# One transformer layer on one core: halves of the array, six warm products, a new order

## The chip, the cores and the metric

The kernel runs on one core of a Trainium2 chip. A core has five engines with a queue each: TensorE (PE, matrix products; its weight loads are shown as PEld), VectorE (DVE), ScalarE (ACT), GpSimd (POOL) and SyncE (SP), whose queue issues most DMAs here. Products write to PSUM, which has eight banks of 128 partitions by 2 KB; everything else lives in SBUF, 128 partitions too. The metric is the time of one execution in microseconds (us) on the device, the median of several runs; lower is better.

## What is computed

One decoder layer in float32, 512 tokens of width 1024, with 256 memory tokens:

```python
h = swiglu(rms_norm(x, ffn1_pre_norm[l]), ffn1_w_gate[l], ffn1_w_up[l], ffn1_w_down[l])
x = x + 0.5 * rms_norm(h, ffn1_post_norm[l])
u = rms_norm(x, mix_pre_norm[l])
...
k_cmp = compress_blocks(kv[:, :, 0], cmp_pos_k[l], cmp_k_w1[l], cmp_k_w2[l])
v_cmp = compress_blocks(kv[:, :, 1], cmp_pos_v[l], cmp_v_w1[l], cmp_v_w2[l])
...
merged = (gates[:, :, 0] * (o_nsa @ w_branch_nsa[l])
          + gates[:, :, 1] * (o_dn @ w_branch_dn[l])
          + gates[:, :, 2] * (o_mem @ w_branch_mem[l]))
x = x + rms_norm(merged @ w_out[l], mix_post_norm[l])
h = swiglu(rms_norm(x, ffn2_pre_norm[l]), ffn2_w_gate[l], ffn2_w_up[l], ffn2_w_down[l])
x = x + 0.5 * rms_norm(h, ffn2_post_norm[l])
```

Three mixers run on the same normed input `u`: an attention in two groups of four heads of 64 (`o_nsa`: over compressed keys, over all causal keys as selected blocks, and over a window; with 512 tokens all eight blocks of 64 are selected and the window reaches all of them), a gated delta rule with four heads of 128 (`o_dn`), and a cross-attention into the memory (`o_mem`). `compress_blocks` is a small network over blocks of 32 tokens: silu of a product with 2048 x 256 weights, once for keys and once for values, then a second product.

## The kernel before

The layer is written out without loops on the device. Most large products are split in two parts of reduced precision, so that one product is three instructions (L117 to L119, helper `mm3`): high by high, low by high, high by low. Each weight tile of 128 x 512 is loaded (L105), cast to its high part on ACT (L106), and its low part is made on DVE or POOL (L109). Small products stay in fp32, and each shows as two instructions in the trace.

The order of work is given by lists of tasks in the dictionary `PRM`: `order_s` for the start of the first FFN, `order0` for its end, `order` for the delta rule and the projections, `order2` for the attention, the memory attention and the merging of the branches, `order3` for the output product and the passage into the second FFN. `tasks` (L1118) walks such a list; a letter names the task and the digits are its arguments. A planner then places each instruction in its engine's queue: among those whose inputs are ready by its own model of time it takes the one that stands earliest in the program. `off` moves a task's instructions ahead by so many places. `order(later, earlier)` tells the planner that one instruction may be placed only after another; it adds no wait on the chip by itself. `pool` says which share of a task's low parts go to POOL. On the chip each engine's queue then runs in the planned order.

These pieces matter here:

- Start: `__init__` fills a tile `wm` with zeros and multiplies it eight times (L61) while the first loads run; the results are not used. `transp` (L190) transposes the first 256 tokens, two feature blocks of 128 at a time (tasks `t00` to `t03`); the tokens come in two halves of 512 features, the second loaded by task `y`.
- Compressed keys: `cmp_in` (tasks `x`), then `cmp_hid` (L927, tasks `p0` to `p7`). Each `p` task loads two weight tiles of 256 KB (L935), one for keys, one for values, from the ring of buffers of the other weights, and makes four products (L940): for two k steps, keys into PSUM partitions 0 to 63 and values into 64 to 127.
- Attention: tasks `S` (`nsa_soft`, L1031) make scores, softmax and the scaling of the probabilities (L217, four per task); tasks `P` (`nsa_pt`, L1054) transpose the probabilities on PE (L1062) and copy them back (L1065); tasks `V` (`nsa_pv`, L1068) multiply them with the values (L1074). A `V` task takes two `P` results, one per group; for each of four key blocks group 0 writes PSUM partitions 0 to 63 and group 1 writes 64 to 127. There are 16 `S`, 16 `P` and 8 `V` tasks. `W` tasks close a pair of heads, `M` tasks merge a branch into the output (`merge_tile`, 36 instructions on PE each).

Of the kernel before, what the change touches and what calls it, by code (L numbers as in the profile page):

```python
# [36 lines left out]
PRM = {'order': ['i', 'a', 'w', 'c01', 'h01', 'r0', 'c00', 'c10', 'c02', 'l0', 'h00', 'h02', 'c12', 'k0', 'h10', 'c22', 'c11', 'h12', 'h11', 'h22', 'r1', 'k1', 'l1', 'b0', 'c21', 'z', 'h21', 'e0', 'c20', 'r2', 'h20', 'c32', 'l2', 'c31', 'd00', 'h31', 'k2', 'r3', 'd01', 'l3', 'b1', 'd02', 'x0', 's00', 'e1', 'd10', 'c30', 'h32', 'x1', 'd11', 'h30', 's01', 's02', 's03', 'q0', 'q3', 'p0', 'o0', 'p1', 'p2', 'p3', 'k3', 'd12', 's10', 'p4', 'q1', 'p5', 's11', 'p6', 'p7', 's12', 's13', 'o1', 'q2', 'f'], 'dma': {'l': 'sync', 'b': 'sync', 'd': 'scalar', 'c': 'sync', 'r': 'sync'}, 'off': {'b0': 300, 'h31': 400, 'r1': 50, 'h32': 50, 'h11': 200, 'h12': 200, 'd10': 100, 'A01': 100, 'A10': 100, 'A11': 100, 'A20': 400, 'A31': 100, 'A21': 20, 'x0': 20, 'x1': 20, 'L': 200, 'S310': 400, 'S001': 20, 'S311': 400, 'A30': 100, 'r0': 400, 'd02': 20, 's11': 100, 'V20': 400, 'l3': 100, 'q1': 20, 'f': 400, 'l1': 20, 'h20': 100, 'h22': 100, 'r3': 50, 'P010': 50, 'y': 100, 'h02': 50, 'S101': 20, 'A00': 100, 'Q0': 50, 'Q1': 200, 'Q2': 50, 'Q3': 50, 'P110': 400, 'V31': 50, 'd01': 200, 'o0': 400, 'p0': 50, 'p1': 50, 'p2': 50, 'p4': 50, 'p5': 20, 'p6': 50, 'p7': 50, 'b1': 200, 'h01': 100, 'M15': 20, 'P201': 400, 'e0': 100, 'e1': 100, 'o1': 20, 'q0': 50, 'q2': 20, 'h21': 20, 'd11': 50, 'p3': 50, 'U0': 100, 's13': 50, 'c11': 20, 's00': 200, 'P011': 400, 'M14': 200, 'c20': 50, 'k2': 20, 'M03': 20}, 'ph': 'e', 'po': 'ss', 'xpd': (0, 1, 2), 'order2': ['K1', 'K0', 'B', 'M10', 'Q0', 'C0', 'Q1', 'S000', 'C3', 'S001', 'P001', 'P000', 'C1', 'S010', 'C2', 'S011', 'V00', 'P010', 'Q2', 'S101', 'S100', 'P011', 'S110', 'V01', 'P100', 'W0', 'P101', 'S111', 'Q3', 'V10', 'P110', 'M12', 'S200', 'P111', 'V11', 'P200', 'S210', 'M14', 'S201', 'M15', 'P201', 'S211', 'W1', 'V20', 'P211', 'P210', 'V21', 'S301', 'S300', 'W2', 'P301', 'S311', 'M11', 'P300', 'L', 'M13', 'S310', 'G0', 'V30', 'P310', 'M16', 'G2', 'P311', 'M17', 'V31', 'W3', 'A00', 'M00', 'A01', 'G1', 'U0', 'M05', 'A10', 'A11', 'G3', 'A30', 'U1', 'A31', 'U3', 'M03', 'M06', 'A20', 'A21', 'U2', 'M07', 'M22', 'M20', 'M02', 'M24', 'M27', 'M21', 'M23', 'M01', 'M04', 'M26', 'M25'], 'order0': ['d0', 'p0', 'n0', 't0', 'd1', 'k2', 'k0', 'p2', 'p3', 'v', 'k3', 'n1', 'k1', 't1'], 'order3': ['s3', 's7', 's2', 's6', 's1', 's5', 's0', 's4', 'd00', 'd01', 'd11', 'g', 'p0', 'n0', 't0', 'd10', 'p1', 'n1'], 't3': (('mm', 'r'), ('e', 's')), 'pool': {'W2': 2, 's13': 3, 'k0': 0, 'k1': 0, 'k2': 0, 'k3': 2, 'p3': 1, 'C0': 1, 'C1': 0, 'C2': 0, 'C3': 2, 'S310': 0, 'L': 3, 'd11': 3, 'p0': 1, 'p1': 1, 'p2': 1, 'p4': 2, 'p5': 1, 'p6': 1, 'p7': 1, 'S311': 0, 'h01': 0, 'h00': 2, 'h02': 0, 'h10': 0, 'h11': 0, 'h12': 0, 'h22': 0, 'h21': 0, 'h20': 0, 'h31': 0, 'h30': 3, 'h32': 0, 'i': 2, 'P011': 2, 'c21': 0, 'd01': 2, 'S000': 0, 'S001': 0, 'S010': 0, 'S011': 0, 'S100': 0, 'S101': 0, 'S110': 0, 'S111': 0, 'S200': 0, 'S201': 0, 'S210': 0, 'S211': 0, 'S300': 0, 'S301': 0, 'M24': 2, 'G2': 2, 'A01': 0, 'M10': 1, 'M15': 2, 'M12': 2, 'M14': 2, 'M13': 2, 'M17': 2, 'M11': 2, 'M16': 2, 'M23': 0, 'M27': 3, 'M01': 2, 'M00': 2, 'M03': 0, 'M07': 2, 'M06': 1, 'M22': 2, 'M04': 2, 'M20': 2, 'M26': 3, 'M02': 0, 'M21': 2, 'M25': 2, 'M05': 2, 'c11': 1, 'o1': 3, 'P000': 2, 'P001': 1, 'P010': 2, 'P100': 2, 'P101': 2, 'P110': 2, 'P111': 2, 'P200': 2, 'P201': 2, 'P210': 2, 'P211': 2, 'P301': 0, 'P300': 2, 'P310': 2, 'P311': 2, 'c12': 0, 'b1': 1, 'x0': 0, 'x1': 0, 'V21': 0, 'c30': 0, 'c01': 0, 'c02': 0, 'c00': 0, 'c10': 0, 'c22': 0, 'c20': 0, 'c31': 0, 'c32': 0, 's01': 3, 'A31': 0, 'd12': 0, 'y': 2, 'G0': 2, 'G1': 2, 'G3': 0, 'U3': 0, 'W3': 2, 'r1': 2, 's12': 3, 'U2': 0, 'Q0': 2, 'Q1': 2, 'Q2': 2, 'Q3': 1, 's00': 3, 's02': 2, 's03': 3, 's10': 2, 's11': 3, 'e1': 2, 'd00': 1, 'U0': 0, 'U1': 0, 'l2': 0, 'd02': 2, 'K1': 3, 'V11': 0, 'V00': 2}, 'pool3': {'d00': 3, 'd01': 3, 'd10': 3, 'd11': 0, 'p1': 2, 't1': 3, 't0': 3, 's5': 2, 's7': 2, 's1': 2, 's0': 2, 's3': 2, 's6': 2, 's2': 2, 's4': 2, 'q0': 1}, 'pool0': {}, 'off0': {'p3': 20, 'n1': 50, 'd0': 200, 'k2': 400, 'k1': 400}, 'off3': {'s1': 20, 's5': 200, 'g': 200, 't0': 400, 'd10': 200, 'p0': 200}, 'tt': ('e', 's'), 'order_s': ['t00', 'w10', 'w00', 'y', 't01', 't02', 'w01', 't03', 'w11', 'R0', 'F000', 'x', 'F101', 'n', 'F200', 't10', 't11', 't12', 't13', 'c', 'F110', 'B', 'F211', 'F011'], 't0': ('e', 's'), 'rs': ((0, 0), (0, 0)), 'ra': (1, 1), 'warm': 8, 'pools': {'F000': 0, 'F101': 0, 'F200': 0, 'F011': 0, 'F110': 0, 'F211': 0, 'w10': 0, 'w11': 0, 't00': 0, 't01': 0, 't02': 0, 't03': 0, 't13': 0, 't10': 0, 't11': 0, 't12': 0, 'w00': 0, 'w01': 0}, 'ptc': 'vvs', 'cva': 'v', 'offs': {'t13': 100, 'R1': 400, 't03': 20, 'w10': 200}, 'vnc': 's', 'sp3': 0, 'hsc': 'vv', 'sf2': 2, 'psc': 'vvvv', 'sp1': 0, 'vbs': 'v', 't1c': 'vs', 'sgv': 256}  # L37


class Body:  # L40
    def __init__(self, ctx, tc, a, out, tap):
# [12 lines left out]
        wm = self.tp.tile([P, 512], BF16, tag="tmpb", bufs=2, name="wm")  # L54
# [4 lines left out]
        pw = self.bank("o", "warm")  # L59
        for _ in range(PRM.get("warm", 10)):  # L60
            nc.tensor.matmul(pw, wm[:, :P], wm, start=True, stop=True)  # L61
# [10 lines left out]


# [139 lines left out]
    def scale(self, eng, out, src, r):  # L213
        if eng == "s":
            self.nc.scalar.activation(out, src, AF.Copy, scale=r)
        else:
            (self.nc.gpsimd if eng == "g" else self.nc.vector).tensor_scalar(out, src, r, None, op0=OP.mult)  # L217
# [709 lines left out]
    def cmp_hid(self, c, Xs, d):  # L927

        nc = self.nc
        if c == 0:  # L930
            d["ph"] = self.bank(PRM.get("ph", "e"), "phid")[:, :256]
        w1 = []
        for which in range(2):
            w = self.wp.tile([P, 2, 256], F32, tag="wraw", name="w1", bufs=self.WB[0])
            nc.sync.dma_start(w, self.a["cmp_w1"][which, c])  # L935
            w1.append(w)
        for k in range(2):
            m = 2 * c + k
            for which in range(2):
                nc.tensor.matmul(d["ph"][64 * which : 64 * which + 64], Xs[which][:, m].rearrange("p g c -> p (g c)"),  # L940
                                 w1[which][:, k], start=m == 0, stop=m == 15)
# [89 lines left out]
    def nsa_soft(self, i, g, br, A, K, tb, sg, ap_):  # L1031
# [20 lines left out]
        return Pm

    def nsa_pt(self, Pm, ap_):  # L1054
        nc, v, te = self.nc, self.nc.vector, self.nc.tensor
        PT = ap_.tile([P, 1280], F32, tag="PT", name="PT", bufs=2)
        for bank, kbs in enumerate(((0,), (1, 3), (2,))):
            pt = self.bank("s", "ppt")
            o = 0
# [8 lines left out]
    def nsa_pv(self, i, br, po, pts, vt):  # L1068
        te = self.nc.tensor
        col = (0, 512, 1024, 896)  # L1070
        for kb in range(TB):
            n = SEQ - kb * P
            for g in range(2):
                te.matmul(po[64 * g : 64 * g + 64, kb * P :], vt[:, kb, br * P + 64 * g : br * P + 64 * g + 64],  # L1074
                          pts[g][:, col[kb] : col[kb] + n], start=br == 0 and kb == 0, stop=False, skip_group_check=True)
# [51 lines left out]
    def run(self):  # L1127
# [3 lines left out]
        with tc.tile_pool(name="f1", bufs=1) as fp, contextlib.ExitStack() as x1:  # L1131
# [13 lines left out]
            def consts():  # L1145
# [76 lines left out]
        with tc.tile_pool(name="mx", bufs=1) as mp:  # L1222
# [293 lines left out]
```

## Time and profile before

| | before |
|---|---|
| median of 3 runs | 1361.38 us |
| lowest and highest | 1360.89, 1362.07 us |
| profiled execution, its own time | 1360.6 us |
| its span, first to last instruction | 1358.8 us |
| PE, DVE, ACT, POOL busy | 98%, 66%, 53%, 10% of the span |
| HBM traffic | 130 GB/s over the span |

The span is what the trace covers; the rest of the execution's time lies around it. A busy PE is not PE at its peak: matrix products are pipelined, so an instruction's time overlaps the next one's, and the step from start to start says what one costs.

### The profile page before, as it was taken

The numbers are of one execution on the slowest core, as the hardware profiler recorded it, in microseconds if no ns is written. First come the engines' busy times: TensorE is split into PE (matmuls) and PEld (weight loads), VectorE is DVE, ScalarE is ACT, GpSimd is POOL, SyncE is SP. The second block draws the span as 40 slices with busy tenths as digits, with TensorE's granted clock in tenths as the row PEclk, the third lists the DMA queues.
The fourth block names the chain that finished last, engine by engine and source line by source line (L and its number), as shares of the span: only waits on it lengthen the run. The fifth ranks groups of instructions, "written<-read, shape, count | busy, mean of one in ns | idle before, by whom it ended". The sixth has DMA issues, their size and how long they took to land.

```text
span 1358.8 us, 21802 instructions
## 1 busy us (share of the span) xinstructions
PE 1330.2 (98%) x7839; PEld 1128.1 (83%) x7839; DVE 899.9 (66%) x1802; ACT 717.7 (53%) x1538; POOL 142.3 (10%) x129
## 2 busy tenths in 40 slices
PE   8999999999999989999999999999999999999997
PEld 7889999788797778787767777788878899998886
DVE  6897876765768775745887323322688778766775
ACT  6566664765655543316655234333576566646652
POOL 0020000000011322003111112323200000000000
PEclk8999999999999999999999999999999999999999
DMA  7543331586664341423111222533744433317773
GB/s 246 194 149 118 100 119 32 178 255 184 210 187 131 83 124 41 126 95 120 52 47 48 78 62 68 189 95 92 257 139 140 135 122 98 121 33 255 199 223 106
DMA packets 107453, 178.32 MB, mean 131 GB/s; under 512 B 18908, under 2 KB 28496, under 8 KB 107344
## 3 DMA queue, kind: packets, MB, share of 16 engines
q1 hardware_dynamic: 107056, 176.67, 41.9%
q8 instruction: 61, 1.00, 0.3%
q14 instruction: 48, 0.39, 0.1%
q10 hardware_dynamic: 288, 0.26, 0.1%
HBM read 166.84 MB, written 10.01 MB: 130 GB/s over the span
## 4 chain that ended last, share of the span: by engine, by line
PE 88%; DVE 5%; ACT 2%; DMA 2%; issue 1%; POOL 0%; SPq 0%; ACTq 0%; DVEq 0%; POOLq 0%
PE smm L429 10%; PE pfm L117 7%; PE pfm L118 7%; PE pfm L119 7%; PE se L429 7%; PE ss L429 3%; PE po L1074 2%; PE ps L1042 2%; PE acc_e L118 2%; PE acc_e L119 2%; PE acc_e L117 2%; PE sr L429 2%; PE acc_s L119 1%; PE acc_s L117 1%; PE acc_s L118 1%; PE so L429 1%
## 5 line engine op out<-in xcount | busy, mean ns | idle before, releaser
L106 ACT CAST whi<-wraw 128x512 fp32r<-128x512 f32 (+1 forms) x314 | 189.8, 614 | 181.4 <-PE pfm L119 65.1
L109 DVE TENSOR_TENSOR wlo<-wraw,whi 128x512 fp32r<-128x512 f32 (+1 forms) x268 | 183.9, 694 | 125.3 <-ACT whi L106 118.2
L117 PE MATMUL pfm<-xth,whi 128*128 128x512 f32 x384 | 154.5, 405 | 3.0 <-DVE cacc L635 3.0
L118 PE MATMUL pfm<-xth,wlo 128*128 128x512 f32 x384 | 154.2, 405 | 1.0 <-POOL wlo L109 1.0
L119 PE MATMUL pfm<-xtl,whi 128*128 128x512 f32 x384 | 154.5, 405 | 0.0
L117 PEld LDWEIGHTS pfm<-xth,whi 128*128 128x128 f32 x384 | 72.4, 189 | 21.0 <-issue 5.2
L119 PEld LDWEIGHTS pfm<-xtl,whi 128*128 128x128 f32 x384 | 72.4, 188 | 16.3 <-issue 2.0
L118 PEld LDWEIGHTS pfm<-xth,wlo 128*128 128x128 f32 x384 | 72.5, 189 | 16.1 <-POOL wlo L109 1.3
L109 POOL TENSOR_TENSOR wlo<-wraw,whi 128x512 fp32r<-128x512 f32 (+1 forms) x43 | 53.6, 1248 | 221.4 <-ACT whi L106 195.2
L106 ACT CAST ringh<-ringr 128x512 fp32r<-128x512 f32 x82 | 50.1, 620 | 42.8 <-PE acc_e L118 8.4
L429 PE MATMUL smm<-thi,fset 128*128 128x256 f32 x384 | 69.4, 279 | 0.0
L109 DVE TENSOR_TENSOR wlo<-ringr,ringh 128x512 fp32r<-128x512 f32 x75 | 51.3, 689 | 21.2 <-PE acc_e L119 6.8
L429 PEld LDWEIGHTS smm<-thi,fset 128*128 128x128 f32 x384 | 58.5, 188 | 0.2
L445 DVE TENSOR_TENSOR up<-smm,s 128x256 f32<-128x256 f32 x32 | 13.6, 424 | 66.5 <-ACT se L442 66.5
L429 PE MATMUL smm<-thi,fxtl 128*128 128x256 f32 x192 | 53.5, 279 | 0.6 <-DVE fxtl L411 0.6
L429 PE MATMUL smm<-thi,fxth 128*128 128x256 f32 x192 | 53.3, 277 | 0.0
L429 PE MATMUL se<-thi,fset 128*128 128x256 f32 x256 | 46.7, 280 | 0.0
L1045 ACT ACTIVATE Pm<-Pm,nm 128x128 f32<-128x128 f32 (+1 forms) x64 | 35.7, 559 | 15.5 <-DVE nm L1044 14.6
L402 DVE TENSOR_TENSOR fs<-fq 128x1024 f32<-128x1024 f32 x32 | 39.0, 1217 | 0.3 <-DMA fq<-in_ffn_u_dram 0.3
L429 PEld LDWEIGHTS se<-thi,fset 128*128 128x128 f32 x256 | 39.1, 187 | 0.0
L123 DVE TENSOR_TENSOR Hl<-H,Hh 128x256 fp32r<-128x256 f32 x88 | 34.9, 420 | 5.6 <-ACT Hh L122 3.7
L1044 DVE CUSTOM_DVE_ANT_0 Pm<-ps,tbl 128x128 f32<-128x128 f32 (+1 forms) x64 | 29.7, 484 | 10.9 <-PE ps L1042 10.3
(565 smaller groups left out, 3946.5 us busy)
## 6 DMA issues: line engine op xcount, KB each, us to landing
wraw<-in_ffn_d_dram SPq DMA_DIRECT2D x94, 256.0 KB, 2.8
ringr<-in_ffn_d_dram SPq DMA_DIRECT2D x82, 256.0 KB, 3.0
fq<-in_ffn_g_dram SPq DMA_DIRECT2D x64, 256.0 KB, 2.8
fq<-in_ffn_u_dram SPq DMA_DIRECT2D x64, 256.0 KB, 2.6
wraw<-in_w_gate_dram SPq DMA_DIRECT2D x48, 256.0 KB, 2.7
wraw<-in_ffn_u_dram SPq DMA_DIRECT2D x34, 256.0 KB, 3.2
wraw<-in_ffn_g_dram SPq DMA_DIRECT2D x34, 256.0 KB, 2.9
woraw<-in_w_out_dram SPq DMA_DIRECT2D x32, 256.0 KB, 3.0
```

What stands on the lines that cost most here:

```text
L106: nc.scalar.copy(hi, raw)
L109: eng.tensor_tensor(lo, raw, hi.bitcast(F32), op=OP.subtract)
L117: t.matmul(out, lh, rh, start=first, stop=False)
L118: t.matmul(out, ll, rh, start=False, stop=False)
L119: t.matmul(out, lh, rl, start=False, stop=last)
L123: return self.nc.vector.tensor_tensor(lo, src, hi.bitcast(F32), op=OP.subtract)
L402: add = lambda *x: v.tensor_tensor(*x, op=OP.add)
L429: m = lambda x, y, **kw: te.matmul(out, x, y, skip_group_check=True, **kw)
L1042: te.matmul(s[:, : max(n, 256)], A[:, qb * P : qb * P + P], K[j][:, : max(n, 256)], start=j == 0, stop=j == 1)
L1044: v.tensor_tensor_reduce(pm, s[:, :n], tb[:, SEQ - n :], -1.0, 3e38, op0=OP.add, op1=OP.min, accum_out=nm[:, qb : qb + 1])
L1045: nc.scalar.activation(pm, pm, AF.Exp, bias=nm[:, qb : qb + 1], scale=-1.0, accum_out=sm[:, qb : qb + 1])
L1074: te.matmul(po[64 * g : 64 * g + 64, kb * P :], vt[:, kb, br * P + 64 * g : br * P + 64 * g + 64], pts[g][:, col[kb] : col[kb] + n], start ...
```

## The change

Four things are edited.

1. `warm` becomes a method, and the zero tile `wm` gets a place of its own. The new task `H6` in `order_s`, between `t01` and `t02`, makes six more of the unused products.
2. In `cmp_hid` the two weight tiles of a chunk come in one load of 512 KB into a tile of their own with two buffers; the host lays the weights out for it.
3. `scale` returns its instruction. `nsa_pt` orders its first transpose after the last scaling of its probabilities, and `nsa_pv` its first product after the last copies of both `P` results.
4. The task lists `order`, `order2` and `order3`, and several offsets and shares for POOL, are set anew.

```diff
-        pw = self.bank("o", "warm")
-        for _ in range(PRM.get("warm", 10)):
-            nc.tensor.matmul(pw, wm[:, :P], wm, start=True, stop=True)
+        self.warm(PRM.get("warm", 10))
...
+    def warm(self, n):
+        p = self.bank("o", "warm")
+        for _ in range(n):
+            self.nc.tensor.matmul(p, self.wm[:, :P], self.wm, start=True, stop=True)
...
-        w1 = []
-        for which in range(2):
-            w = self.wp.tile([P, 2, 256], F32, tag="wraw", name="w1", bufs=self.WB[0])
-            nc.sync.dma_start(w, self.a["cmp_w1"][which, c])
-            w1.append(w)
+        w1 = d["cm"].tile([P, 2, 2, 256], F32, tag="w1", name="w1", bufs=2)
+        nc.sync.dma_start(w1, self.a["cmp_w1"][c])
...
-        return Pm
+            q = self.scale(PRM.get("psc", "vvvv")[qb], pm, pm, sm[:, qb : qb + 1])
+        return Pm, q
...
+                    if not bank and not o and PRM.get("gp", 1):
+                        self.order(q, after)
...
+                if not kb and not g and PRM.get("gv", 1):
+                    for p in pts:
+                        self.order(q, p[1])
...
+                "H": self.warm,
```

In `PRM` the lists change in these places (offsets: what was, what is; none means zero):

```
order    c11 c22 ahead of h12 (was c22 c11); c21 h21 b0 e0 z (was b0 c21 z h21 e0);
         k2 ahead of l2 (was behind h31); s01 ahead of h30; q3 p0 d12 o0 p1 q0 p2
         (was q0 q3 p0 o0 p1 p2 .. d12 behind k3)
order_s  H6 between t01 and t02
order2   P000 ahead of C3, P010 ahead of C2, M12 ahead of P100, S200 S210 ahead of V10,
         W2 ahead of S300, P301 behind P300, P310 behind M17, A31 U3 ahead of U1, M25 ahead of M04
order3   s2 and s5 earlier, d10 ahead of n0
off      V00 V01 V10 V11 V21 V30: none to 400; V31: 50 to 400
         p1 p2 p3 p4 p6 p7: 50 to 400; p5: 20 to 400
         h00 none to 400; l2, P101 none to 200; i none to 100; h11 200 to 100; l1 20 to 50;
         G0, S210, G2 none to 20
off0     d0 200 to none; k1 400 to 20; p0 none to 400; p2 none to 100
off3     t0 400 to 200; n0 none to 200
```

More of the change, by code (lines that the diff above doesn't have):

```diff
@@ L53, in __init__ @@
         nc = self.nc
-        wm = self.tp.tile([P, 512], BF16, tag="tmpb", bufs=2, name="wm")
+        self.wm = wm = self.sp.tile([P, 512], BF16, name="wm", bufs=1)
         nc.vector.memset(wm, 0.0)
@@ L214, in scale @@
         if eng == "s":
[L215 removed]
+            return self.nc.scalar.activation(out, src, AF.Copy, scale=r)
         else:
[L217 removed]
+            return (self.nc.gpsimd if eng == "g" else self.nc.vector).tensor_scalar(out, src, r, None, op0=OP.mult)
     def rowscale(self, xs, tbs, RB, engs, tag, after=None):
@@ L940, in cmp_hid @@
                 nc.tensor.matmul(d["ph"][64 * which : 64 * which + 64], Xs[which][:, m].rearrange("p g c -> p (g c)"),
-                                 w1[which][:, k], start=m == 0, stop=m == 15)
+                                 w1[:, k, which], start=m == 0, stop=m == 15)
     def compress(self, ph, cm, op_):
@@ L1061, in nsa_pt @@
                 for qb in range(kb, TB):
-                    te.transpose(pt[:, o : o + P], Pm[:, self.OFF[qb] + kb * P : self.OFF[qb] + kb * P + P], self.ident)
+                    q = te.transpose(pt[:, o : o + P], Pm[:, self.OFF[qb] + kb * P : self.OFF[qb] + kb * P + P], self.ident)
+                    if not bank and not o and PRM.get("gp", 1):
+                        self.order(q, after)
                     o += P
             dst = PT[:, bank * 512 : bank * 512 + o]
-            (nc.scalar.copy if PRM.get("ptc", "svs")[bank] == "s" else v.tensor_copy)(dst, pt[:, :o])
-        return PT
+            q = (nc.scalar.copy if PRM.get("ptc", "svs")[bank] == "s" else v.tensor_copy)(dst, pt[:, :o])
+        return PT, q
     def nsa_pv(self, i, br, po, pts, vt):
@@ L1236, in run @@
             with tc.tile_pool(name="cm", bufs=1) as cmp_, tc.tile_pool(name="da", bufs=1) as self.da, tc.tile_pool(name="dn", bufs=1) as dp:
-                st, ys, Xs, R, E, sc = [{} for _ in range(4)], {}, {}, [{}, {}], {}, []
+                st, ys, Xs, R, E, sc = [{} for _ in range(4)], {}, {}, [{}, {}], {"cm": cmp_}, []
                 def small():
@@ L1458, in host_layout @@
     a["cmp_pos"] = np.stack([i[f"cmp_pos_{s}"][0].reshape(16, P).T for s in "kv"])
-    a["cmp_w1"] = np.stack([i[f"cmp_{s}_w1"][0].reshape(8, 2, P, 256).transpose(0, 2, 1, 3) for s in "kv"])
+    a["cmp_w1"] = np.stack([i[f"cmp_{s}_w1"][0].reshape(8, 2, P, 256) for s in "kv"]).transpose(1, 3, 2, 0, 4)
     a["cmp_w2"] = np.stack([i[f"cmp_{s}_w2"][0].reshape(2, P, 64).transpose(1, 0, 2) for s in "kv"])
```

8 lines of the change are left out of this document (4 added, 4 removed).

## The prediction

> **What bounds the kernel now.** I read the page first: how busy each engine is, and which engine carries the chain that ended last.
>
> ```profile
> PE 1330.2 (98%) x7839; PEld 1128.1 (83%) x7839; DVE 899.9 (66%) x1802; ACT 717.7 (53%) x1538; POOL 142.3 (10%) x129
> PE 88%; DVE 5%; ACT 2%; DMA 2%; issue 1%; POOL 0%; SPq 0%; ACTq 0%; DVEq 0%; POOLq 0%
> ```
>
> TensorE (PE) is busy 98% of the span of 1358.8 us and carries 88% of the chain. Only two things can shorten such a kernel: PE's own work, or the little idle time between. So next come the stretches the change touches, in the view by windows (columns: length, then busy time of PE, weight loads, DVE, ACT, POOL; then granted clock, share of DMA, GB/s). 400 to 660 us is the mixer up to the compressed keys, 660 to 785 the attention, 960 to 1020 the passage into the second FFN.
>
> ```profile
> 400.00:660.00 260.00, 250.87 (x1434) 204.14 (x1434) 172.64 (x468) 116.92 (x282) 52.80 (x53) 1.00 0.35 101
> 660.00:785.00 125.00, 125.00 (x653) 88.21 (x652) 82.48 (x258) 61.42 (x171) 17.97 (x14) 1.00 0.18 54
> 960.00:1020.00 60.00, 56.84 (x316) 47.92 (x315) 45.44 (x108) 42.23 (x87) 6.46 (x5) 1.00 0.58 186
> ```
>
> In the attention PE is never idle, while DVE has 42.5 us free of 125: what PE saves there is saved. In the mixer PE idles 9.1 us, at the passage 3.2 us.
>
> **Part 1, the attention's products with the values (L1074).** One call of nsa_pv (a V task) issues for each of four key blocks one product per group; group 0 writes PSUM partitions 0 to 63, group 1 writes 64 to 127, so each uses half of the array's columns. Each fp32 product shows as two instructions, so a V task has 16. The windows below hold one V task each, for the instructions of L1074 alone (columns: length, PE busy, weight loads busy, clock, DMA, GB/s).
>
> ```profile
> 660.00:669.00 9.00, 3.87 (x16) 1.27 (x16) 1.00 0.12 36
> 672.00:681.00 9.00, 3.65 (x16) 1.37 (x16) 1.00 0.09 29
> 690.00:697.00 7.00, 3.65 (x16) 1.35 (x16) 1.00 0.34 90
> 697.00:706.00 9.00, 3.65 (x16) 1.35 (x16) 1.00 0.14 47
> 720.00:724.00 4.00, 2.37 (x16) 1.06 (x16) 1.00 0.20 62
> 726.00:730.00 4.00, 2.37 (x16) 1.06 (x16) 1.00 0.00 0
> 757.00:761.00 4.00, 2.37 (x16) 1.06 (x16) 1.00 0.22 67
> 776.00:784.00 8.00, 3.66 (x16) 1.15 (x16) 1.00 0.21 66
> ```
>
> The same 16 instructions take 2.37 us in three tasks and 3.65 to 3.87 us in five. In the three they stand in one run, and the two halves of the array work at once; in the five, other work is queued between them, and a product without its partner has half the array for itself. The change adds an order: the first product of a V task is placed only after the last copies of both groups' transposed probabilities, and every V task gets an offset of 400, ahead of nearly everything. Then all eight should be one run. The five then save 18.48 - 5 x 2.37 = 6.63 us.
>
> Each run also has edges. The timeline of PE at a run of two (start, length, line), with two ordinary products of the same width behind it:
>
> ```profile
> 666.92 0.39 PE L1042 MATMUL ps<-KL,qa 128*128 128x512 f32 x1
> 667.24 0.43 PE L1074 MATMUL po<-PT,big 128*64 128x128 f32 x2
> 667.60 0.50 PE L119 MATMUL pfm<-xtl,whi 128*128 128x512 f32 x1
> 667.94 0.39 PE L117 MATMUL pfm<-xth,whi 128*128 128x512 f32 x1
> ```
> ```profile
> 573.29 0.40 PE L118 MATMUL pfm<-xth,wlo 128*128 128x512 f32 x1
> 573.53 0.39 PE L119 MATMUL pfm<-xtl,whi 128*128 128x512 f32 x1
> ```
>
> An ordinary start-to-start step is 573.53 - 573.29 = 0.24 us. Into the run it is 0.32, out of it 0.34 for the first product behind: 0.08 + 0.10 more. The run's busy 0.43 reaches 0.07 beyond the next start (667.60), so an edge pair costs 0.11 us over the busy time. By the timeline there are 19 runs now (four in the first task, three in each of the other four that are cut, one in each whole one); 8 remain; 11 x 0.11 = 1.2 us. Part 1 gives 6.6 + 1.2 = **7.8 us**. Its ends: 0, if the tasks stay cut, and 7.8, since nothing is faster than the whole runs of 2.37.
>
> What the waits cost: the order added in nsa_pt holds a P task's first transpose until all four scalings of its probabilities (L217) are done, and PE's queue is in order, so scores, merge products and all that stand behind would wait with it. The groups of the window 660 to 785 (columns: busy us, mean ns):
>
> ```profile
> L217 DVE TENSOR_SCALAR Pm<-Pm,smx 128x512 f32<-128x512 f32 x14 | 6.7, 481 | 0.0
> L217 DVE TENSOR_SCALAR Pm<-Pm,smx 128x384 f32<-128x384 f32 x14 | 5.8, 414 | 0.0
> L217 DVE TENSOR_SCALAR Pm<-Pm,smx 128x256 f32<-128x256 f32 x14 | 4.9, 348 | 0.0
> L119 PE MATMUL pfm<-xtl,whi 128*128 128x512 f32 x58 | 23.4, 404 | 0.0
> ```
>
> The wait is 0.35 + 0.41 + 0.48 = 1.24 us at most (the second to fourth scaling), sixteen times. I cost it at nothing: its cover is merge products, 58 of this one form alone in the stretch, at steps of 0.24 us, which the order lets PE take meanwhile. Without that cover it costs 16 x 1.24 = 19.8 us; that is a rival below. The wait in nsa_pv adds nothing that its data didn't ask for.
>
> **Part 2, the compression's hidden layer (L940).** Here too keys write partitions 0 to 63 and values 64 to 127: 32 products, 64 instructions. First row: windows, L940 alone; then PE's timeline; last, from the view of the tile w, the idle time of PE before its products.
>
> ```profile
> 562.00:601.00 39.00, 13.14 (x64) 5.13 (x64) 1.00 0.41 121
> ```
> ```profile
> 589.90 0.65 PE L940 MATMUL phid<-w,X 128*64 128x256 f32 x4
> ...
> 592.41 0.65 PE L940 MATMUL phid<-w,X 128*64 128x256 f32 x2
> ```
> ```profile
> 599.36 1.08 PE L940 MATMUL phid<-w,X 128*64 128x256 f32 x6
> ```
> ```profile
>   DMA w<-in_cmp_w_dram: 0.8, 2
> ```
>
> Four instructions of a pair take 0.65 us, the same as two of a product alone; six (a pair and one alone) take 1.08, as a pair and a pair would. Now there are 15 runs. The change fetches keys' and values' weights of one chunk in one load, so all 8 instructions of a p task come ready at once, and p1 to p7 have an offset of 400. Eight runs at 1.08 make 8.64: 13.14 - 8.64 = 4.5 us, and 7 edges x 0.11 = 0.8: 5.3 us. If each task is still cut between its two pairs, 16 x 0.65 = 10.4 remain and the gain is 2.7 - 0.1 = 2.6 us. The load is now 512 KB with two buffers in place of four of 256 KB; PE waited 0.8 us for these loads, and I let that wait double: 5.3 - 0.8 = **4.5 us**, range 0 to 5.3. Of the loads that stay, those of the weight ring get two buffers back, which I cost at nothing, PE being the pacer.
>
> **Part 3, six products between the transposes.** The clock in windows of 3.41 us, cut where the granted clock changes (4.85, 8.26, 15.08); the first two rows, from elsewhere, hold the longest gap of PE. Then PE's timeline at the start.
>
> ```profile
> 503.14:506.56 3.42, 1.89 (x9) 1.19 (x7) 3.38 (x6) 0.00 (x0) 0.21 (x1) 1.00 0.30 89
> 506.56:509.97 3.41, 1.96 (x11) 1.69 (x12) 3.38 (x7) 1.68 (x5) 0.00 (x0) 1.00 0.71 220
> 4.85:8.26 3.41, 1.25 (x8) 0.84 (x8) 0.88 (x3) 1.21 (x3) 0.00 (x0) 1.00 0.88 256
> 8.26:11.67 3.41, 2.49 (x12) 2.52 (x13) 1.49 (x5) 1.51 (x4) 0.00 (x0) 0.50 1.02 366
> 11.67:15.08 3.41, 3.41 (x18) 3.41 (x18) 3.01 (x6) 2.97 (x6) 0.00 (x0) 0.50 1.00 399
> ```
> ```profile
> 1.19 3.59 PE L61 MATMUL warm<-wm 128*128 128x512 bf16 x8 [1.19 <-DVE wm L55]
> ```
> ```profile
> 5.92 1.25 PE L198 MATMUL ptr<-cst,xa 128*128 128x128 f32 x8 [1.14 <-DMA xa<-in_x_dram]
> ...
> 9.18 0.66 PE L198 MATMUL ptr<-cst,xa 128*128 128x128 f32 x2 [2.01 <-DMA xa<-in_x_dram]
> ```
>
> A window in which PE is busy 1.25 of 3.41 us (37%) is followed by half clock until 15.08; two of 55% and 57% kept full clock. A warm product took about 0.43 us (8 in 3.59) before the clock rose, so about 0.21 at full clock, an estimate. Six placed behind the eight transposes last 1.3 us, from about 7.0 to 8.3, inside the idle 2.01 us that end at 9.18; the window is then 1.25 + 1.2 = 2.45 of 3.41 busy, 72%, and I expect full clock from there. PE's 5.90 us of work to 15.08 would need 2.95 less at most; but from 11.67 on ACT (2.97), DVE (3.01) and the DMA (1.00) are nearly full, so I count the first window only: 2.49 / 2 = **1.3 us**. Ends: 2.9, and a loss of 0.4, if the six run at half clock (6 x 0.43 = 2.6, from 7.0 to 9.6, past 9.18).
>
> The Trainium skill, "TensorE: Matmul & The Clock Gate", Part 4, says that transposes do not count as busy for the clock gate. By that rule only the six products would count, 1.3 of 3.41 us, 38%, and the gain would be nothing. The trace has a drop at 37% and holds at 55%, both counted with all PE work, and does not decide it.
>
> **Part 4, the order.** In the mixer z moves behind b0 and e0, c11 ahead of c22, h21 and d12 forward, q0 back; in the attention P310 moves behind M17, M12 forward; ahead of w_out and into FFN 2 s2 and d10 forward; and offsets change. With a c, q or z its weight loads move past others on SP's queue, with an l or k its products on POOL. Nothing is added. The largest single wait there is PE's for DVE in a convolution:
>
> ```profile
> PE pfm L117 <- DVE cacc L635: 3.0, 1, 3.0
> ```
>
> What order can win is bounded by the idle time it finds, 9.1 + 3.2 = 12.3 us, and it can lose as much by new waits. Nothing in the trace says which. I take 0, and 4 us either way for the range, about this longest wait and one short one. The tile wm of its own and the returned handles cost nothing; the six products have bank "o", which only PE writes until then.
>
> **Sum.** 7.8 + 4.5 + 1.3 + 0 = 13.6 us. The profiled execution took 1360.6 us (span 1358.8, and 1.8 around it), so it becomes 1347.0; the median of the runs shown is 0.8 above it, 1361.4, so the forecast is **1347.8 us**.
>
> **The rivals.**
> (a) *The saved PE time turns into waits*: between 540 and 625 us the delta rule's chain over DVE needs filling, and the shorter L940 fills less; or p tasks, drawn together, wait for 512 KB loads. Against it: PE idles only 0.4 us from 560 to 600 now. About half would be left: 1361.4 - 6.8 = 1354.6.
> (b) *Slower*: the wait for all four scalings finds no cover, in 660 to 785. At its full 19.8 us the time is 1347.8 + 19.8 = 1367.6. It turns the sign from 13.6 / 16 = 0.85 us a P task on, over two thirds of the wait. Against it: PE's 125.0 of 125.
> (c) *The change does not do what it says*: the runs stay cut, as the order only tells the planner and the run differs; nothing of parts 1 and 2: 1361.4 - 1.3 = 1360.1.
> (d) *The clock falls at 8.26 all the same*: the nearest row that fell had 37%; part 3 gives nothing: 1349.1. By the Trainium skill's rule on transposes this is what comes.
>
> **How the numbers follow.** Forecast 0.56, (a) 0.20, (d) 0.13, (c) 0.06, (b) 0.05. A measurement of this kernel tells 0.2%, 2.7 us, from no change. Faster: forecast, (a), (d): 0.89; same: (c), 0.06; slower: (b), 0.05. The low end takes part 2 whole, the clock whole and 4 us of order: 1347.8 - 0.8 - 1.6 - 4 = 1341.4. The high end reaches to (a), 1354.6. That leaves out (b), (c) and the tails.
>
> **What would show it.** Right: eight runs of 16 at L1074, each 2.37 us; L940 at about 8.6 us in eight runs of 8; granted clock 1.00 at 8.26. Wrong: L1074 runs shorter than 16 (part 1, rival c); PE idle before L1062 (rival b); PE idle before L940 on its load, or more than 9.1 us idle from 400 to 660 (rival a, or order); 0.50 at 8.26 (rival d). What would make it wrong most likely is part 4, the one term without a row.

## The result, and the profile after

The kernel with the change takes **1345.88 us** (median of 4 runs, 1345.23 to 1347.03), the one before 1361.14 (4 runs, 1359.14 to 1362.07). The ratio is 0.9891, its 95% interval 0.9874 to 0.9908: 15.3 us less, 12.5 to 17.2 by the interval. The forecast was 1347.8 us with a range of 1341.4 to 1354.6. Ratios below are to the kernel before, timed on the same chip, with their 95% intervals. In one experiment (the old mixer list) four of ten runs show a mean granted clock of 0.982 to 0.983 where the other six have 0.994 to 0.998, and take 1366.4 us or more; these four are set aside there.

First the page of the kernel after: busy time of each engine, and the chain that ended last.

```profile
span 1345.2 us, 21803 instructions
...
PE 1318.5 (98%) x7845; PEld 1125.8 (84%) x7845; DVE 903.2 (67%) x1804; ACT 712.1 (53%) x1536; POOL 140.4 (10%) x127
...
PE 87%; DVE 5%; DMA 3%; ACT 3%; issue 2%; POOL 0%; SPq 0%; DVEq 0%; ACTq 0%
```

PE's busy time fell by 11.7 us (1330.2 to 1318.5) and the span by 13.6; the share stayed at 98%. It is the same kind of kernel as before, with less work on PE. The windows of the same three stretches (length, then busy time of PE, weight loads, DVE, ACT, POOL; granted clock, share of DMA, GB/s):

```profile
400.00:660.00 260.00, 250.94 (x1473) 206.68 (x1472) 182.95 (x490) 118.81 (x293) 50.03 (x51) 1.00 0.34 98
660.00:785.00 125.00, 125.00 (x662) 92.63 (x662) 81.50 (x247) 61.29 (x168) 18.60 (x15) 1.00 0.20 60
960.00:1020.00 60.00, 56.88 (x351) 49.35 (x350) 52.37 (x117) 45.95 (x92) 2.57 (x2) 1.00 0.48 152
```

In 400 to 660 us PE is idle 9.06 us (it was 9.13), in the attention it has no idle time, as before, and at the passage 3.12 us (3.16). But 39 more PE instructions fit into the first window (1473 against 1434): the gain is work done sooner, not waiting removed.

Now the two sets of products that stand in half arrays. The products with the values are L1078 in the kernel after (L1074 before); this is the windows view for that line alone (PE busy, weight loads busy, clock, DMA, GB/s):

```profile
650.00:785.00 135.00, 19.00 (x128) 8.50 (x128) 1.00 0.20 59
```

The 128 instructions take 19.00 us, 2.375 for each of the eight tasks, and PE's timeline shows eight runs of 16. Before, the same 128 took 25.61 us, the sum of the eight windows shown in the prediction (25.59) within rounding. The hidden layer of the compression (L940), windows view for that line alone, then PE's timeline (start, length, line):

```profile
562.00:601.00 39.00, 8.45 (x64) 3.97 (x64) 1.00 0.39 117
```
```profile
565.00 1.95 PE L940 MATMUL phid<-w,X 128*64 128x256 f32 x16
569.86 1.08 PE L940 MATMUL phid<-w,X 128*64 128x256 f32 x8
...
584.44 1.08 PE L940 MATMUL phid<-w,X 128*64 128x256 f32 x8
```

One run of 16 and six of eight, 8.45 us where it was 13.14, and no idle time stands before any of them. The waits of PE in 400 to 660 us (total, times, longest):

```profile
PE ptk L681 <- DVE qs L674: 2.7, 2, 1.6
PE ptk L681 <- DVE kn L674: 1.7, 1, 1.7
PE ptk L681 <- DVE Bi L747: 1.6, 1, 1.6
...
PE pfm L120 <- DVE cacc L638: 0.3, 1, 0.3
```

The wait of 3.0 us for DVE in a convolution is down to 0.3, and others have come in its place: the idle time changed its owner, not its size.

Along PE's timeline the gain builds up in three stages. The first FFN's last product into `acc_s` ends 0.93 us earlier than before (375.60 against 376.53). The last product of the compressed keys ends 5.83 us earlier (598.53, was 604.36), so some 5 us came from the mixer. The attention's last product into `po`, one with the compressed values (L1308, L1300 before), ends 13.64 us earlier (780.82, was 794.46), so some 8 us came from the attention. Nothing is added or lost behind it: the span is 13.56 us shorter.

The first of these stages can't be read from one execution. In the seven traces whose first FFN is that of the kernel after, it ends between 372.19 and 375.60 us; in the five that have the one of the kernel before, between 375.09 and 376.53. The kernel after's own trace is the latest of its seven. What lies behind the first FFN differs less: from its end to PE's last product the trace takes 962.25 us in the kernel after, and 962.77 and 961.80 in the kernels of experiments 5 and 3, which do the same work there; it takes 974.64 in the kernel before.

Last, the start. PE's timeline of the kernel after (L75 are the products on zeros, L201 the transposes; in brackets the idle time before), and its windows of 3.41 us:

```profile
1.19 3.60 PE L75 MATMUL warm<-wm 128*128 128x512 bf16 x8 [1.19 <-DVE wm L55]
5.99 1.08 PE L201 MATMUL ptr<-cst,xa 128*128 128x128 f32 x4 [1.21 <-DMA xa<-in_x_dram]
6.87 1.06 PE L75 MATMUL warm<-wm 128*128 128x512 bf16 x2
7.73 1.06 PE L201 MATMUL ptr<-cst,xa 128*128 128x128 f32 x4
8.58 1.30 PE L75 MATMUL warm<-wm 128*128 128x512 bf16 x4
```
```profile
5.72:9.13 3.41, 3.14 (x12) 2.28 (x13) 0.44 (x2) 0.95 (x3) 0.00 (x0) 1.00 0.82 260
9.13:12.54 3.41, 3.41 (x28) 3.00 (x27) 2.96 (x8) 2.73 (x8) 0.00 (x0) 1.00 1.01 377
```

The six products stand as two and four, not behind all eight transposes, and the first of them run at half clock: two take 0.86 us from start to start (6.87 to 7.73), and four transposes 0.85 (7.73 to 8.58). The trace's first record of the granted clock is 1.00 from 9.13 on; the 1.00 of the first row is only the view's value where no record lies. From 9.13 the DMA is full (1.01 of its share, 377 GB/s).

### The profile page after: what moved, and what is told of

Same layout as the page of the kernel before. It is cut to its first block, busy times and chain, and to the rows that moved or that the text cites. A ratio compares the mean times of both kernels' runs of the same rounds, so it can differ in the third digit from the quotient of the medians.

```text
span 1345.2 us, 21803 instructions
## 1 busy us (share of the span) xinstructions
PE 1318.5 (98%) x7845; PEld 1125.8 (84%) x7845; DVE 903.2 (67%) x1804; ACT 712.1 (53%) x1536; POOL 140.4 (10%) x127
## 4 chain that ended last, share of the span: by engine, by line
PE 87%; DVE 5%; DMA 3%; ACT 3%; issue 2%; POOL 0%; SPq 0%; DVEq 0%; ACTq 0%
PE smm L432 10%; PE pfm L120 8%; PE pfm L122 7%; PE pfm L121 7%; PE se L432 7%; PE ss L432 3%; PE acc_s L122 2%; PE acc_s L121 2%; PE acc_s L120 2%; PE ps L1042 2%; PE sr L432 2%; DVE wlo L112 1%; PE so L432 1%; PE acc_e L121 1%; PE acc_e L122 1%
## 5 line engine op out<-in xcount | busy, mean ns | idle before, releaser
L112 DVE TENSOR_TENSOR wlo<-wraw,whi 128x512 fp32r<-128x512 f32 x270 | 188.2, 705 | 109.5 <-ACT whi L109 104.2
L432 PE MATMUL smm<-thi,fset 128*128 128x256 f32 x384 | 69.5, 279 | 0.0
L432 PEld LDWEIGHTS smm<-thi,fset 128*128 128x128 f32 x384 | 58.5, 188 | 0.2
L448 DVE TENSOR_TENSOR up<-smm,s 128x256 f32<-128x256 f32 x32 | 13.6, 424 | 66.8 <-ACT se L445 66.8
L432 PE MATMUL smm<-thi,fxtl 128*128 128x256 f32 x192 | 53.6, 279 | 0.6 <-DVE fxtl L414 0.6
L432 PE MATMUL smm<-thi,fxth 128*128 128x256 f32 x192 | 53.3, 278 | 0.0
L432 PE MATMUL se<-thi,fset 128*128 128x256 f32 x256 | 46.7, 280 | 0.0
L432 PEld LDWEIGHTS se<-thi,fset 128*128 128x128 f32 x256 | 39.1, 187 | 0.0
L432 PEld LDWEIGHTS smm<-thi,fxtl 128*128 128x128 f32 x192 | 36.0, 188 | 1.0 <-DVE fxtl L414 1.0
```

The lines of the kernel that those rows point to most:

```text
L112: eng.tensor_tensor(lo, raw, hi.bitcast(F32), op=OP.subtract)
L432: m = lambda x, y, **kw: te.matmul(out, x, y, skip_group_check=True, **kw)
L448: v.tensor_tensor(up[:, 256:], a, s7, op=OP.add)
```

## The experiments

Twelve kernels were run. In the expectations, theory A is what I held at that point and theory B its rival; each text says what they mean there. Edits of a list or an offset are given in words, and a line number belongs to the kernel named.

**1. The two halves apart.** In the kernel after, the eight products of one group come first, then those of the other.

```diff
-        for kb in range(TB):
-            n = SEQ - kb * P
-            for g in range(2):
+        for g in range(2):
+            for kb in range(TB):
+                n = SEQ - kb * P
```

> The changed kernel, but each V task makes all four products of group 0 first and then all four of group 1: the same 16 instructions, still in one run, but a product's neighbour is in the same half of the array. Theory A (the two halves work at once only when products of both stand side by side): each run has its eight products one after the other, 4.27 us of steps in place of 2.13, so about 4.5 us busy in place of 2.37; eight times 2.13 is 17.1 us, 1363.0 us in all. Theory B (what costs is each entry into and exit from such a run, and the change saves by having 8 runs in place of 19): nothing changes, 1345.9 us.

Measured: 1358.66 us (10 runs), ratio 0.9987 (0.9978 to 0.9997), 12.8 us over the kernel after. Windows view of L1078 alone, then one task on PE's timeline:

```profile
640.00:800.00 160.00, 31.43 (x128) 14.47 (x128) 1.00 0.17 54
```
```profile
655.57 3.93 PE L1078 MATMUL po<-PT,big 128*64 128x512 f32 x16
```

The runs are still eight of 16, at the same places in the queue, and each takes 3.93 us instead of 2.38. The busy time is 12.43 us longer (31.43 - 19.00), about what the whole kernel lost. So it isn't standing in one run that saves the time, but the partner in the other half as a neighbour. The expected 4.5 us a task was too much because the two groups still meet at the seam: the first product of the second group starts at 657.131 us, 6 ns behind the third of the first.

**2. No order edges.** The kernel after with `gp` and `gv` set to 0: the offsets of 400 and the lists stay, the two calls of `order` go.

> The changed kernel without the two order edges, of P and of V; all offsets of 400 and the new lists stay. The planned queue then has the V products in 19 runs again in place of 8. Theory A (the edges make the runs whole): by the steps of the products (0.85, 0.64, 0.43, 0.21 us for key blocks 0 to 3, halves at once only inside a run, 0.35 us of edge a run) 28.4 us in place of 19.9, so 8.5 us more, 1354.4 us. Theory B (the offsets and the new lists carry the gain): within 1 us of 1345.9. Theory C (the order on the first transpose costs waits of up to 1.24 us a P task): faster than theory A by up to 19.8 us, that is, well under 1354.

Measured: 1355.31 us (5 runs), 0.9965 (0.9950 to 0.9980), 9.4 us over the kernel after. Windows view of L1078 alone:

```profile
640.00:800.00 160.00, 26.07 (x128) 10.67 (x128) 1.00 0.18 56
```

The products fall apart into 19 runs and 26.07 us, as before the change. That is 7.1 of the 9.4 us; PE also idles 1.5 us from 660 to 785, where it didn't idle at all. The edges do it; the offset alone lets the planner draw each product forward as soon as its own copy is ready.

**3. No edge on the transposes.** As above, but `gp` alone is 0: the first transpose need not stand behind the four scalings.

> The changed kernel without the order on a P task's first transpose; that of V stays, and the planned V runs are still eight of 16 instructions. Theory A (the wait for the last scaling is covered by merge products and costs nothing): within 1 us of 1345.9; a little above, if the transposes' runs, cut more often in the planned queue (54 in place of 46), cost an edge each of about 0.1 us. Theory B (the wait costs PE time, up to 1.24 us a P task): faster than 1345.9 by more than 2 us.

Measured: 1345.36 us (4 runs), 0.9891 (0.9874 to 0.9907), the same as the kernel after. L1078 still takes 19.00 us. The wait for the last scaling costs nothing, and the edge on the transposes brings nothing either; the one on the products is the one that counts.

**4. Two loads per chunk.** The kernel after, with keys' and values' weights in two loads and two tiles of 256 KB, two buffers each.

```diff
-        w1 = d["cm"].tile([P, 2, 2, 256], F32, tag="w1", name="w1", bufs=2)
-        nc.sync.dma_start(w1, self.a["cmp_w1"][c])
+        w1 = []
+        for which in range(2):
+            w = d["cm"].tile([P, 2, 256], F32, tag=f"w1{which}", name="w1", bufs=2)
+            nc.sync.dma_start(w, self.a["cmp_w1"][which, c])
+            w1.append(w)
```

> The changed kernel with the weights of a p task in two loads of 256 KB again, keys' and values' each into a tile of its own with two buffers; offsets and lists stay. In the planned queue six of the eight tasks are then cut into 1 + 3 products. Theory A (one load makes the products ready together, and that is what pairs them): six times 0.43 us for the product alone and 0.35 for the edge, 4.7 us more, 1350.5 us, with L940 at about 12 us busy in place of 8.45. Theory B (the two buffers it gives back to the weight ring, or the offsets, carry the gain): within 1 us of 1345.9.

Measured: 1349.72 us (4 runs), 0.9924 (0.9907 to 0.9940), 3.8 us over the kernel after. Windows view of the hidden layer's line (L943 here) alone:

```profile
562.00:601.00 39.00, 12.29 (x64) 5.04 (x64) 1.00 0.36 105
```

13 runs (a run of 16, then six times two and six), 3.84 us more than 8.45: the whole difference. Under the new order, a task whose four products come ready by one load is worth what its runs say.

**5. No six products.** The kernel after without `H6` in `order_s`.

> The changed kernel without the six products. Theory A (they keep or raise the clock early): the granted clock is 0.50 in the first 15 us for some 6 us of PE's work, the first Strassen product starts about 1.3 us later, 1347.0 us. Theory B (the first stage is bound by loads and by ACT, and the clock makes nothing of it): within 0.4 us of 1345.9.

Measured: 1345.78 us (4 runs), 0.9894 (0.9879 to 0.9909): no difference that these runs can show, as each ratio is good to some 2 us. Its windows:

```profile
3.85:7.26 3.41, 1.38 (x9) 0.68 (x8) 0.69 (x1) 0.14 (x1) 0.00 (x0) 1.00 0.84 242
7.26:10.67 3.41, 2.41 (x12) 2.04 (x11) 2.32 (x5) 2.09 (x5) 0.00 (x0) 0.50 0.99 357
10.67:14.08 3.41, 3.41 (x18) 3.41 (x17) 2.21 (x5) 2.69 (x7) 0.00 (x0) 0.50 1.02 401
```

Without them the clock is 0.50 until 14.08, with them it is full from 9.13. From 7.26 on the DMA is full in this kernel too (0.99 and 1.02 of its share). The product that starts at 17.43 without the six starts at 16.14 with them, 1.3 us earlier. By 20 us half of this lead is gone, 0.4 us of it where PE waits for a low part made by DVE. Then PE has hardly any idle time, and the first product of the FFN's next stage (L432, into `smm`, the expectation's first Strassen product) starts at 70.33 without and at 69.71 with them, 0.6 us apart. The trace is one execution of each. Over all fourteen traces that product starts at 69.70 us on average in the eight with the six products (68.92 to 70.32) and at 70.38 in the six without (69.79 to 71.19). So some 0.7 us may be gained at the start, and the times of whole executions can't tell it from nothing.

**6. Part 1 alone.** The kernel before with the two edges, and an offset of 900 for all `V` tasks (which puts each of them in one run under the old lists).

> The kernel before with part 1 alone: the two order edges, and an offset of 900 for the V tasks (400 leaves one of them cut in the old lists). In the planned queue all eight V tasks are whole. Theory A (whole runs are worth 7.8 us wherever the rest of the order stands): 1360.7 - 7.8 = 1352.9 us, L1074's products at 19.0 us busy in eight runs. Theory B (the gain needs the new lists around it, since the V tasks now hold back other work): less than 4 us gained, above 1357.

Measured: 1355.12 us (5 runs), 0.9960 (0.9944 to 0.9976), 6.0 us faster than before. Windows view, the products with the values alone (L1081 here), then all instructions in the attention's stretch:

```profile
640.00:800.00 160.00, 19.00 (x128) 8.46 (x128) 1.00 0.21 64
```
```profile
660.00:785.00 125.00, 124.11 (x673) 90.87 (x673) 83.16 (x257) 61.88 (x173) 19.58 (x15) 1.00 0.18 56
```

All 6.6 us of busy time are saved, and 0.89 us comes back as idle time where there was none.

**7. Part 2 alone.** The kernel before with the one load into two buffers of its own, and the offsets of 400 for `p1` to `p7`.

> The kernel before with part 2 alone: one load for a chunk's two weight tiles, two buffers, offset 400 for p1 to p7. The planned queue has L940 in nine runs in place of 15, one task still cut. Theory A (PE time saved is time saved): by 0.43 us a step and 0.35 us an edge 4.7 us, 1356.0 us. Theory B (the saved time turns into waits of PE for the 512 KB loads or for the delta rule's chain): half of it or less, 1358.4 us or more, with idle time of PE before L940 or more than 9.1 us idle from 400 to 660 us.

Measured: 1360.82 us (10 runs), 1.0000 (0.9991 to 1.0009): nothing. Windows view of L940 alone; SP's queue; PE at the fifth task's products; and the window behind it:

```profile
560.00:601.00 41.00, 9.93 (x64) 4.19 (x64) 0.96 0.35 110
```
```profile
562.98 1.19 SPq L936 DMA_DIRECT2D w<-in_cmp_w_dram  x2
564.26 0.38 SPq L108 DMA_DIRECT2D wraw<-in_w_k_dram  x1
570.21 0.38 SPq L752 DMA_DIRECT2D Dc<-dD  x1
570.69 6.69 SPq L936 DMA_DIRECT2D w<-in_cmp_w_dram  x3
```
```profile
575.82 1.19 PE L940 MATMUL phid<-w,X 128*64 128x256 f32 x8 [2.96 <-DMA w<-in_cmp_w_dram]
```
```profile
576.67:580.08 3.41, 3.41 (x12) 1.41 (x10) 2.80 (x12) 0.00 (x0) 0.00 (x0) 0.50 0.57 199
```

All tasks but one stand in one run and 3.2 us of busy time are saved (13.14 to 9.93), half clock included. But the third and fourth weight loads (the rows at 562.98; the first two were issued at 343.9 and 353.3) are followed in SP's queue by the load of `Dc` (L752), which brings the delta rule's blocks back from DRAM. SP issues nothing from 564.64 to 570.21. The fifth weight load needs the buffer that the third task's products leave at 568.10; it goes out behind `Dc` at 570.69, 2.6 us later, and PE waits 2.96 us for it. Then PE runs 3.41 us at half clock. Idle time in 400 to 660 us grew from 9.13 to 12.90.

**8. Part 2 alone, with `Dc` on another queue.** The same with the load of `Dc` issued by ACT (`'dma': {'c': 'scalar'}`).

> Part 2 alone on the kernel before (as in the run of part 2 alone), with one more edit: the load of Dc, which waits for the delta rule's blocks to come back through DRAM, is issued by ACT and no longer by SP, where it stood between the second and the third weight load of the p tasks. Theory A (PE's waits of 3.4 us for these loads come from SP's queue standing still behind Dc, and the low clock after the long wait costs up to 1.7 us more): the waits and the dip of the clock are gone, L940 has seven runs, and part 2 is worth its 4.7 us, about 1356 us. Theory B (two buffers of 512 KB are too few, or the loads too slow): the waits before L940 stay, 1360 us or more. Theory C (the delta rule's chain lacks filling): no wait before L940, but idle time elsewhere from 400 to 660 us, over 11 us in all, 1359 us or more.

Measured: 1364.78 us (6 runs), 1.0029 (1.0017 to 1.0041), slower than before. ACT's timeline, then DVE's, then PE's:

```profile
572.14 0.42 ACTq L752 DMA_DIRECT2D Dc<-dD  x1
572.60 0.28 ACT L843 ACTIVATE sq<-pod 128x128 bf16<-128x128 f32 x1 [3.14 <-DMA dD<-Bi]
```
```profile
576.90 0.69 DVE L765 TENSOR_TENSOR Dm<-Dc,msk 128x512 f32<-128x512 f32 x1 [9.37 <-DMA Dc<-dD]
```
```profile
582.00 0.74 PE L850 MATMUL pot<-cst,on 128*128 128x128 f32 x2 [4.08 <-DVE on L849]
```

The fifth weight load now goes out at 570.20, as soon as its buffer is free, and PE doesn't wait for it; 0.35 us of wait before the fourth task is left. So the place behind `Dc` was what held that load (the fifth; the expectation counts from the row at 562.98). But now ACT stands 3.14 us, until the store that `Dc` reads back has landed, with the delta rule's squares (L843) behind it. DVE stands 9.37 us for `Dc` itself: its first step on `Dc` (L765) now comes ahead of the steps that lead to L849, three of which stood ahead of it in experiment 7. The squares are done at 574.97, so it is `Dc` that DVE waits for last; L849 starts at 581.59, and PE waits 4.08 us for it. The wait for the store has only moved to other queues.

**9. All parts under the old order.** Edges, one load and six products, with the lists of before, `V` at 900 and `p1` to `p7` at 400.

> All of parts 1, 2 and 3 with the old task lists and old offsets (V tasks at 900, p tasks at 400): the change without its new order. The planned queue has nine V runs and nine of L940, two and two more... one and two more than the changed kernel. Theory A (the order by itself is worth nothing): 1345.9 + 1.5 for those three runs = 1347.4 us. Theory B (the new order is worth what the measured gain has over the sum of the parts, about 1.7 us, and more if part 3 is worth nothing, as the run without the six products says): 1349 to 1350.5 us.

Measured: 1355.57 us (4 runs), 0.9960 (0.9945 to 0.9975): 5.5 us gained of the 15.3. Waits of PE, and the two stretches by windows:

```profile
PE pfm L120 <- DVE cacc L638: 3.0, 1, 3.0
PE phid L940 <- DMA w<-in_cmp_w_dram: 2.3, 2, 2.0
```
```profile
400.00:660.00 260.00, 248.15 (x1423) 202.53 (x1423) 170.34 (x466) 115.88 (x279) 51.99 (x52) 0.99 0.32 97
660.00:785.00 125.00, 123.48 (x666) 88.77 (x665) 84.86 (x258) 61.97 (x173) 18.18 (x14) 1.00 0.18 56
```

Idle time is 11.85 us in the first stretch (9.06 in the kernel after) and 1.52 in the second (0.00). Neither theory had this: given the parts, the order with its offsets and shares for POOL is worth 9.7 us (1355.57 - 1345.88; 9.4 by the ratios).

**10. The old order with the new mixer list.** The kernel of experiment 9 with the new `order`; `H6`, of which experiment 5 could measure nothing, is left out.

> All of parts 1, 2 and 3 with the old attention list and offsets (V at 900), and the new list of the mixer alone. Theory A (the mixer's list is worth 5 us and the attention's list the other 4.4 us of the difference that the stages show): 1355.6 - 5 = 1350.6 us. Theory B (the lists only count together): above 1353. Theory C (the mixer's list is the whole of it): 1347 us or less.

Measured: 1351.16 us (4 runs), 0.9934 (0.9917 to 0.9950), 4.4 us faster than experiment 9 by the medians, 3.5 by the ratios, each good to some 2 us.

**11. The kernel after with the old mixer list.** Only `order` is put back.

> The changed kernel with the old list of the mixer alone (order); the attention's list, the one after it and all offsets are the new ones. The planned queue has nine runs of L940 in place of seven, one task cut, and all V runs whole. Theory A (of the new order it is the mixer's list that matters, as it keeps the p tasks' loads out from behind Dc): PE waits 2 to 3.5 us before L940 and some 5 us are lost, 1351 us. Theory B (the attention's list carries it): within 1.5 us of 1345.9, those for the two runs more.

Measured: 1351.35 us (6 runs, 1350.07 to 1354.46), 0.993 of the kernel before by the medians, so 5.5 us over the kernel after. Waits of PE:

```profile
PE pfm L120 <- DVE cacc L638: 3.0, 1, 3.0
...
PE phid L940 <- DMA w<-in_cmp_w_dram: 0.9, 1, 0.9
```

The convolution's wait of 3.0 us is back with the list, and with it a wait for `w`, of 0.9 us. So the mixer list carries some 3.5 to 5.5 us of the order's 9.7, by experiments 10 and 11. The traces from the end of the first FFN to PE's last product, where the six products and the start play no part, take 962.25 us in the kernel after, 971.45 in experiment 9, 965.48 in 10 and 967.66 in 11: by them it is 5.4 to 6.0 of 9.2 us. The attention's list and the offsets carry the rest.

**12. The kernel after with `Dc` on ACT's queue.**

> The changed kernel with the load of Dc issued by ACT. Theory A (in the new order nothing waits behind Dc any more): within 1 us of 1345.9, with L940 in seven runs as before and the same 9 us idle from 400 to 660 us. Theory B (SP's queue still holds back loads that PE needs, in the run with the old loads or in others): 1 to 3 us faster.

Measured: 1350.23 us (4 runs), 0.9925 (0.9910 to 0.9939), 4.4 us over the kernel after. Neither theory had that. Waits of PE in 400 to 785 us:

```profile
PE pt L787 <- DVE Dm L765: 3.1, 1, 3.1
...
PE pot L850 <- DVE on L849: 1.4, 2, 1.1
```

The planner lays the other queues anew when a load changes its engine, so this doesn't price ACT's queue by itself; it shows that the new lists fit SP's queue with `Dc` in it. There, the load of `Dc` is issued at 567.60, right behind two weight loads that end at 567.31. The next weight load has no free buffer before 570.94 and goes out at 571.30, and PE doesn't wait for it.

No kernel of these is measurably faster than the kernel after.

## Why the prediction came true, point by point

**The bound.** Right. PE stayed at 98%, and time went only where its own work got shorter or where a wait was met.

**Part 1 (7.8 us).** The mechanism is shown by experiments 1 and 2, and the term of 6.63 us inside the runs came out at 6.61 (25.61 - 19.00). By itself the part brought 6.0 us. The term for the edges, 1.2 us worked out from one run of two, was mis-sized: nothing of it is seen. From the end of the first FFN on, PE's busy time fell by 6.02 us (961.57 to 955.55), less than the runs' own 6.61. A run behind an ordinary product started 0.32 to 0.33 us after it; the whole runs of the kernel after start 0.40 to 0.41 after it, and why is open. That the four scalings find their cover was right (experiment 3), and with it rival (b) is out.

**Part 2 (4.5 us).** The runs came out as forecast, 8.45 us against 8.64. The wait of 0.8 us was read too high: the view gives 0.3 of it to PE and 0.5 to PE's weight loads. It didn't grow under the new order, and under the old one PE's grew to 3.4. There the part is worth 0 (experiment 7), so rival (a) was a true account of that order: PE waits for the 512 KB loads. What I had not seen is why: not only the time that a load takes and the two buffers, but the `Dc` ahead of it in SP's queue, which kept the fifth load back for 2.6 us. Under the new order the one load is worth 3.8 us (experiment 4).

**Part 3 (1.3 us).** Not confirmed: the time shows nothing (experiment 5), but it couldn't have told 1.3 us from nothing for sure. The clock does become full earlier, at 9.13 instead of 15.08, and the first product into `smm` starts 1.27 us earlier than before. But it starts at 69.81 us in the kernel with part 2 alone, which has no six products, and at 70.32 in experiment 1, which has them: single starts vary by as much. The averages over the traces leave some 0.7 us, so the term was about twice too large. I had let the full DMA limit only the second window; the row of the first, 8.26 to 11.67, had it too (1.02). I had also placed the six behind all eight transposes and expected the clock not to fall at 8.26; in this execution it hadn't risen yet.

**Part 4 (0, with 4 us either way).** This is the step that failed: it prices the order apart from the parts. By its bound of idle time it looked right: the idle time from 400 to 660 didn't change. What the bound can't see is that the parts would have added idle time under the old order. There parts 1 to 3 bring 5.5 us of the 13.6 I summed (experiment 9), and the new order brings the other 9.7. Booked so, the sum came out within 2 us by two errors, +8.1 in parts 1 to 3 and -9.7 in part 4. It can be booked the other way too. Taken out of the kernel after one at a time, the edges are worth 9.4 us, the one load 3.8 and the six products nothing measurable: 13.2 us, near the 13.6, and at the start, in the mixer and in the attention the kernel after gained 0.9, 4.9 and 7.8 us, where the sum had 1.3, 4.5 and 7.8. So the parts are worth what the prediction says in an order that lets them come through, and some 7 to 8 us belong to parts and order together. That the new order is such a one was taken for granted and stood in no row: so far the number was luck.

**The rivals.** (a) holds for the old order and not for the new. (b) is out by experiment 3. (c) is out: the runs are whole. (d), that the clock gives nothing, is neither shown nor out: the time shows no gain, but the clock was full early.

**What stays open.** Which of the moves in the attention's lists and the offsets carry the remaining 3 to 6 us was not separated. The profiled executions of experiment 10 and of the kernel after are 2.9 us apart (spans 1348.1 and 1345.2), and 2.3 of it is idle time of PE: 0.91 us from 660 to 785, where the kernel after has none, and 10.49 against 9.06 from 400 to 660. The new order without the parts was not run, nor `Dc` on POOL's queue. The first FFN ends some 2 us earlier on average in the traces that have the six products and the new offsets of its end; which of the two does it wasn't separated.

## What to carry to other kernels

When work on the bounding engine is to shrink, look in the queues beside it for what its old length covered: a load whose place is behind one that waits for a round trip through DRAM is hidden only as long as the work ahead of it lasts. Price a reordering together with the edits it comes with, and test them both ways, the parts under the old order and the order with one part taken out; an idle time that stays the same says nothing of what the order is worth. Products in two halves of the array save time only with the partner as the next product in the queue, so ask for an edge that holds back the first of them until the data of all are ready.

## What the runs showed of the hardware

**The clock.** In all traces the granted clock changes only at points a whole number of 3.41 us apart, and where these lie differs from run to run; the six products are met by another phase each time. In the start the last change to full clock lies at 4.06 to 10.52 us in the eight traces with them, and at 11.75 to 15.08 in the six without. The window ahead of a change decides, and transposes count in it. One such window is that of the kernel after from 5.72 to 9.13, shown above; the other is of experiment 1, by the same view:

```profile
0.28:3.69 3.41, 2.50 (x6) 0.89 (x7) 0.27 (x1) 1.82 (x3) 0.49 (x7) 1.00 0.43 132
```

The first, 3.14 us busy of which 1.61 are products, is followed by full clock. The second, 2.50 us of products alone, is not: the next transposes still step by 0.21 us. If only products counted, 1.61 could not do what 2.50 can't. The Trainium skill, "TensorE: Matmul & The Clock Gate", Part 4, says that a transpose doesn't count as busy in the same way; these windows speak against it, though the trace doesn't show whether the transpose mode that the page describes was on. In the fourteen traces, windows of up to 2.51 us busy of 3.41 didn't raise the clock and those from 2.66 did. Full clock was lost behind windows of up to 1.59 us busy and held behind all from 1.61, but also behind one of 1.50 (experiment 7, 504.99 to 508.40), so this second limit isn't sharp.

**A wait of 3 us in the middle.** The same wait of 3.0 us for `cacc` cost no clock before, as it fell over two windows of 1.89 and 1.96 us busy. In experiment 9 it lay within one, and the next window ran at half clock:

```profile
502.40:505.81 3.41, 0.75 (x3) 0.63 (x4) 3.34 (x6) 0.86 (x2) 0.00 (x0) 1.00 0.73 217
505.82:509.23 3.41, 3.41 (x11) 2.83 (x10) 2.50 (x5) 1.74 (x9) 0.00 (x0) 0.50 0.38 132
```

Half clock for 3.41 us costs up to 1.7 us (an estimate, half of the window), so a wait of this length can cost half as much again, by chance of the phase.

**The issuing engine.** The Trainium skill, "DMA: Bandwidth & Descriptors", section "Issuing engines are not separate DMA queues", says that issuing from several engines saves only the sequencer's issue time. For bandwidth no run here speaks against it. For a load that waits for data it matters more than that: `Dc` issued by SP held the weight load behind it by 2.6 us, and PE waited 2.96 us for that load. Issued by ACT it held ACT 3.14 us, and DVE, which needs `Dc`, stood 9.37 us and PE 4.08.
